# Moving the weight sums, the last batch's close, the memory tokens' split and two orders in a hybrid decoder layer

## The chip, the core and the metric

The kernel runs on one core of one Trainium2 chip. The metric is the device time of one execution in microseconds (us), the median of several runs. The engines are named as the profile does: PE is TensorE (PEld its weight loads), DVE is VectorE, ACT is ScalarE, POOL is GpSimd, SP is SyncE, whose queue issues most DMAs. "L825" is line 825 of the kernel before.

## What is computed

One layer of a decoder for 1024 prompt tokens and 8 sample requests of 4 tokens, each with 4096 cached tokens in 128-token pages. It has a mixer (gated MLP and latent attention side by side, one output projection), a cross-attention into 256 memory tokens, and a gated ConvFFN:

```python
def mla_keys_values(ckv_n, kpe, pos, w_uk, w_uv, g_qk_k):
    lead = ckv_n.shape[:-1]
    k_nope = (ckv_n @ w_uk).reshape(*lead, MLA_HEADS, QK_NOPE)
    v = (ckv_n @ w_uv).reshape(*lead, MLA_HEADS, V_HEAD)
...
def merge_out(a_out, b_out, g_out_a, g_out_b, w_o):
    return jnp.concatenate([rms_norm(a_out, g_out_a), rms_norm(b_out, g_out_b)], axis=-1) @ w_o

def mem_kv(mem, g_mem_in, w_mk, w_mv, g_mk):
    n, m, _ = mem.shape
    hm = rms_norm(mem, g_mem_in)
    k = rms_norm((hm @ w_mk).reshape(n, m, MEM_HEADS, MEM_HEAD_DIM), g_mk)
    v = (hm @ w_mv).reshape(n, m, MEM_HEADS, MEM_HEAD_DIM)
    return k, v
...
def conv_ffn(h, buf, w_up, w_conv, b_conv, w_down):
    t = h.shape[1]
    gate, val = jnp.split(h @ w_up, 2, axis=-1)
    gpad = jnp.concatenate([buf.astype(gate.dtype), gate], axis=1)
    conv = b_conv + sum(gpad[:, j:j + t] * w_conv[j] for j in range(CONV_W))
    return (jax.nn.silu(conv) * val) @ w_down, gpad[:, t:]
```

Products are made to fp32 precision: each operand is split into a high and a low part ("h", "l"), and `mm3` multiplies high by high, low by high and high by low.

## The kernel before

**Stages.** By the trace: input projections to about 200 us; attention over the prompt (`phase2a`) to 418; attention of the sample requests over their pages (`phase2b`) to 883; the memory keys (`mem_kv`) with the last request's softmax and output to 927; the output projection to 1100; memory attention to 1190; the ConvFFN to 1873.

**Prompt attention.** It has 16 units (head h, half G of the tokens), cut into 56 steps t. Tables say which side work is recorded in which step: `extra[t]` holds the splits of raw weights (`split_w`), the preparations of heads (`preps`: ropes on POOL, L609 to L612, the k addition L910, transposes L933), projections that come late, the sample queries' preparation (`sample_prep`: memsets of bdq and cn on POOL, L1039 and L1040, ahead of a copy of cn on ACT and its transposes on PE, L980), the output normalisation of the prompt (`mix`) and the 26 weight sums. PE, ACT, DVE and POOL run in the order that the tables give; SP's order comes from the scheduler.

**Weight sums.** The ConvFFN multiplies two-by-two blocks with seven products, which needs sums of weight blocks. `weight_sums` (L812) makes them ahead of time: load 512 KB (L817 or L822), four subtractions and additions on POOL (L825 to L828), store 512 KB (L829). Four sums take `w_up`, 22 take `w_down`. All use two buffers "wsum", which first hold the raw `w_uq` and `w_uv` halves that `split_w` reads; a buffer takes its next load when its last reader is done. In the tables the sums stand at steps 7 to 11, 25 to 31 and 36 to 50.

**Sample attention.** Each step loads pages (cT on L1311, ck on L1315), and POOL's krq product (L1330) feeds the first scores. The last steps also hold `mem_split`: the first four of eight blocks of memory tokens are scaled and split (ACT L195, DVE L198) while pages are still worked on. `mem_kv` then splits the other four inside head 0 and makes the keys of four heads. Three functions close each request: `batch_out` twice and `batch_close`, which ends in an ACT copy into `olT` (L1483). Those of the last request are called from `end()`, within the output projection, after `mixed` has recorded the splits (mx1, mx2: ACT L195, DVE L198) of the mixer's output for column blocks 1 and 2.

**ConvFFN.** A gate block's product X is drained by DVE into z (L2114) and into G (L2138); the convolution's steps run on DVE (L2161, L2162) into cv.

Of the kernel before, what the change touches and what calls it, by code (L numbers as in the profile page):

```python
# [6 lines left out]
FR = mybir.dt.float32r  # L7
# [6 lines left out]
P = 128  # L14
# [140 lines left out]
class Net:  # L155
# [23 lines left out]
    def mm3(self, out, a, b, first=True, last=True):  # L179
# [4 lines left out]
        for i, (l, r) in enumerate(seq):  # L184
            self.nc.tensor.matmul(out, l, r, start=first and i == 0, stop=last and i == len(seq) - 1)  # L185

    def split(self, hi, lo, src, g=None, eng="act"):

        nc = self.nc
        if g is None:  # L190
            {"act": nc.scalar.copy, "pool": nc.gpsimd.tensor_copy, "dve": nc.vector.tensor_copy}[eng](hi, src)  # L191
            low = lambda: nc.vector.tensor_tensor(lo, src, hi, ALU.subtract)  # L192
        else:
            if eng == "act":
                nc.scalar.activation(hi, src, AF.Copy, scale=g)  # L195
            else:
                {"pool": nc.gpsimd, "dve": nc.vector}[eng].tensor_scalar(hi, src, g, None, ALU.mult)
            low = lambda: nc.vector.scalar_tensor_tensor(lo, src, g, hi, ALU.mult, ALU.subtract)  # L198
        if self.lows is None:
            low()  # L200
        else:
            self.lows.append(low)

    def flush(self):
# [443 lines left out]
    def phase2a(self):  # L648
# [68 lines left out]

        put(split_w, (4, 5, 6, 7))
        spread(tok_s, 4, 11)
# [402 lines left out]
    def phase2b(self):  # L1122
# [47 lines left out]
        at(last - 4, 3, lambda: self.split(*wk0, raws[0].rearrange("p (k n) -> p k n", k=8)))  # L1170
        mem0 = []

        def mem_split(k):
            if k % 2 == 0:
                x = self.t(p, [P, 4, 288], FR, "ck", 15).rearrange("p k n -> p (k n)")[:, :1024].rearrange("p (k z n) -> p k z n", k=2, z=2)
                mem0.extend((x[:, e, 0], x[:, e, 1]) for e in range(2))
            self.split(*mem0[k], raws[1].rearrange("p (k n) -> p k n", k=4)[:, k], self.col("g_mem_in", k))

        for k in range(4):
            at(last - 3 + k, 3, mem_split, k)  # L1180
        for b in range(NB):
# [22 lines left out]
        def steps(n0, n1):  # L1204
            for n in range(n0, n1):
# [6 lines left out]
                for k, dst, src in ((1, b4, self.b_dram), (16, self.fold4, I["c_fold4"]), (64, wuv, I["w_uv"])):  # L1212
                    if n == k:
                        self.tc.add_manual_dep(
                            nc.sync.dma_start(dst, src).ins, self.page_dma[-1].ins.name,
                            mybir.DependencyInfo(mybir.DependencyClass.NoSync, mybir.DependencyReason.DATA), reason="order",
                        )
                if n > last - 8 and n % 2 == 0 and len(raws) < 4:
# [29 lines left out]
        with tc.manual_schedule(engines={E.SP}):  # L1248
            self.close("ps3")
            for x in ("p3a", "p3c", "sq", "sm"):  # L1250
                self.close(x)
            self.wr = self.open("wr", bufs=3, side="right")
            self.wp = self.open("w", bufs=3, side="right")
            mem = self.mem_kv(raws, wk0, mem0)
            for f in late:
                f()
            for _ in range(12):
                next(mem)
            steps(last + 1, last + 16 + LAG)
            for _ in mem:  # L1260
                pass
        self.close("p3")

        def end():
            for f in tail:
                f()
            ps = self.t(ppt, [P, 512], F32, "m", 1)[:NS]
            for h in range(8):
                for k in range(2):
                    nc.tensor.matmul(  # L1270
                        ps[:, h * 64 : h * 64 + 64], self.olT[:, k, h].rearrange("p b t -> p (b t)"),
                        wuv[:, k, h * 64 : h * 64 + 64], start=k == 0, stop=k == 1,
                    )
# [3 lines left out]
        return end  # L1277

# [199 lines left out]
    def batch_close(self, p, pp, b, s):  # L1478
        nc = self.nc
        tp = s["tp"][:, :64]  # L1480
        for k in range(2):
            nc.tensor.matmul(tp[:, k * 32 : k * 32 + 32], s["oo"][:, k * P : k * P + P], self.fold4[:, :32], start=True, stop=True)
        nc.scalar.copy(self.olT[:, :, :, b], tp.rearrange("p (k h t) -> p k h t", k=2, h=8))  # L1483

# [14 lines left out]

    def mem_kv(self, raws, wk0, mem0):  # L1500

# [5 lines left out]
        st = self.t(pp, [P, 512], F32, "st", 1)  # L1507
        mh, ml = (self.t(p, [P, 4, 256], FR, x) for x in ("mh", "ml"))
# [114 lines left out]

    def mixed(self):

# [464 lines left out]
    def ffn_up(self, ops, rows, norm, first):  # L2090
# [40 lines left out]
        def gate(w, fs, h, prev):  # L2131
# [24 lines left out]
            for e, f in enumerate(fs):  # L2156
# [176 lines left out]
def build(tc, I, O, stop=99, tap=None):  # L2333
# [22 lines left out]
    if done(2):  # L2356
        return
    end = N.phase2b()
    if done(3):
        return  # L2360
    mxs, ws = N.mixed()
    xp = N.open("x", side="right")
# [49 lines left out]
```

## Time and profile before

| what | us |
|---|---|
| median of 3 runs | 1878.63 |
| lowest and highest | 1877.48, 1888.89 |
| the profiled execution | 1874.82 |
| its span in the profile | 1873.1 |
| PE busy in the span | 1816.2 |
| DVE, ACT, POOL busy | 1347.5, 927.7, 693.9 |

By stage, from windows of the trace:

| stretch, us | PE busy | granted clock |
|---|---|---|
| 0 to 200 | 196.44 | 1.00 |
| 200 to 428 | 200.64 | 0.93 |
| 428 to 883 | 451.07 | 0.99 |
| 883 to 927 | 36.23 | 0.92 |
| 927 to 1100 | 170.04 | 0.99 |
| 1100 to 1190 | 85.83 | 1.00 |
| 1190 to 1873 | 675.95 | 1.00 |

A stretch's length less PE's busy time is idle time of PE; a granted clock below 1 means that its matmuls ran slower for a part of the stretch. The stretches with the most of both are the second and the fourth.

### The profile page before, as it was taken

Reading aid. Unit: us, or ns where it says so; the run is one execution under the profiler, and the core shown is the slowest. Engines: PE = TensorE matmul, PEld = TensorE weight load, DVE = VectorE, ACT = ScalarE, POOL = GpSimd, SP = SyncE. Lnnn points to the kernel's source line nnn. Section 1 sums busy time; section 2 is a strip of 40 time slices with the busy share of each in tenths; the row PEclk is TensorE's granted clock in tenths of the full one; section 3 lists DMA queues with packets and bytes.
Section 4 is the critical chain, followed back from the end, with each engine's and each line's share of the span. In section 5 each row is a group of like instructions: output and inputs, shape, how many; then the busy total and the mean of one; then the engine's idle time right before and its main releaser. Section 6 shows DMA issues by size and latency. Waiting matters only on the chain.

```text
span 1873.1 us, 39347 instructions
## 1 busy us (share of the span) xinstructions
PE 1816.2 (97%) x14222; PEld 1710.1 (91%) x14222; DVE 1347.5 (72%) x2796; ACT 927.7 (50%) x1965; POOL 693.9 (37%) x850
## 2 busy tenths in 40 slices
PE   9999899888999999998899999999999999999999
PEld 8999677658999999998799988899999999999999
DVE  7855666555887667777644676888888888878664
ACT  7436677555555555555433455633333333344442
POOL 1022244544444444544213110267776677500000
PEclk9999999798999999999999999999999999999999
DMA  8101042578776676664554345422222222495242
GB/s 322 38 25 66 21 136 82 191 239 233 217 199 188 176 199 185 171 177 141 153 160 134 127 158 151 132 67 80 81 83 90 69 74 75 114 350 166 79 154 76
DMA packets 153187, 261.18 MB, mean 139 GB/s; under 512 B 20897, under 2 KB 97538, under 8 KB 152994
## 3 DMA queue, kind: packets, MB, share of 16 engines
q1 hardware_dynamic: 152130, 257.63, 44.6%
q8 instruction: 112, 1.84, 0.4%
q10 hardware_dynamic: 864, 1.05, 0.2%
q14 instruction: 81, 0.66, 0.1%
HBM read 212.79 MB, written 45.82 MB: 138 GB/s over the span
## 4 chain that ended last, share of the span: by engine, by line
PE 76%; issue 6%; DMA 5%; SPq 4%; DVE 4%; POOL 3%; ACT 1%; DVEq 0%; POOLq 0%; ACTq 0%
PE s L185 12%; PE d L185 12%; PE mm L185 9%; PE b L185 7%; PE F L185 7%; PE X L185 7%; PE E L185 7%; PE A L185 3%; PE y L185 3%; SPq L1311 2%; SPq L1315 2%; PE o L995 1%; PE tp L185 1%; PE tp L980 1%; DMA wsumd<-wsum 1%
## 5 line engine op out<-in xcount | busy, mean ns | idle before, releaser
L185 PE MATMUL s<-w2h,ch 128*128 128x288 f32 (+1 forms) x1024 | 304.7, 298 | 0.5 <-ACT S L1361 0.5
L185 PE MATMUL s<-w2h,cl 128*128 128x288 f32 (+1 forms) x1024 | 296.8, 290 | 3.3 <-POOL cl L1343 3.3
L185 PE MATMUL s<-w2l,ch 128*128 128x288 f32 (+1 forms) x1024 | 295.5, 289 | 0.0
L185 PEld LDWEIGHTS s<-w2h,ch 128*128 128x128 f32 x1024 | 193.6, 189 | 8.9 <-ACT sq L1383 2.5
L185 PEld LDWEIGHTS s<-w2h,cl 128*128 128x128 f32 x1024 | 193.2, 189 | 5.4 <-POOL cl L1343 5.4
L185 PEld LDWEIGHTS s<-w2l,ch 128*128 128x128 f32 x1024 | 193.8, 189 | 0.0
L1386 DVE TENSOR_REDUCE ss<-sq 128x16 f32<-128x1024 f32 x128 | 155.3, 1213 | 32.5 <-ACT sq L1383 32.1
L1343 POOL TENSOR_TENSOR cl<-cT,ch 128x512 fp32r<-128x512 f32 x64 | 82.8, 1294 | 128.0 <-ACT ch L1339 127.1
L1383 ACT ACTIVATE sq<-s 128x512 f32<-128x512 f32 x128 | 76.5, 598 | 89.3 <-PE s L185 89.3
L1380 ACT ACTIVATE sq<-s 128x512 f32<-128x512 f32 x128 | 76.7, 599 | 73.6 <-PE s L185 72.7
L191 ACT CAST a<-brb 128x528 fp32r<-128x528 f32 x77 | 48.8, 634 | 112.9 <-PE d L185 108.5
L185 PE MATMUL d<-a,w 128*128 128x264 f32 x768 | 95.4, 284 | 1.2 <-DVE G L2185 1.2
L192 DVE TENSOR_TENSOR a<-brb,a 128x528 fp32r<-128x528 f32 x77 | 54.2, 705 | 57.4 <-ACT a L191 57.4
L185 PEld LDWEIGHTS d<-a,w 128*128 128x128 f32 x768 | 94.3, 188 | 1.3 <-issue 1.3
L2055 POOL TENSOR_TENSOR lo<-s,hi 128x1024 fp32r<-128x1024 f32 x20 | 62.8, 3142 | 45.4 <-ACT hi L2054 45.4
L185 PE MATMUL mm<-wlo,xh 128*128 128x256 f32 (+3 forms) x272 | 77.0, 286 | 0.1
L185 PE MATMUL mm<-whi,xh 128*128 128x256 f32 (+3 forms) x272 | 77.0, 285 | 0.0
L185 PE MATMUL mm<-whi,xl 128*128 128x256 f32 (+3 forms) x272 | 76.9, 287 | 0.0
L2110 ACT COPY a<-A 128x264 f32<-128x264 f32 x43 | 16.1, 374 | 118.8 <-PE A L185 113.9
L1339 ACT CAST ch<-cT 128x512 fp32r<-128x512 f32 x128 | 73.4, 626 | 0.0
L185 PE MATMUL d<-a,hi 128*128 128x264 f32 x552 | 72.0, 284 | 0.0
L1382 DVE TENSOR_TENSOR S<-s,S 128x64 f32<-128x64 f32 x128 | 28.0, 219 | 60.5 <-ACT sq L1380 60.4
(757 smaller groups left out, 6402.2 us busy)
## 6 DMA issues: line engine op xcount, KB each, us to landing
cT<-cT SPq DMA_DIRECT2D x256, 160.0 KB, 2.9
ck<-ck SPq DMA_DIRECT2D x256, 144.0 KB, 3.5
raw<-w_up SPq DMA_DIRECT2D x44, 512.0 KB, 3.6
wsumd<-wsum SPq DMA_DIRECT2D x26, 512.0 KB, 3.4
actd<-cv SPq DMA_DIRECT2D x44, 264.0 KB, 2.4
brb<-actd SPq DMA_DIRECT2D x44, 264.0 KB, 5.6
wsum<-w_down SPq DMA_DIRECT2D x22, 512.0 KB, 3.9
raw<-wsumd SPq DMA_DIRECT2D x20, 512.0 KB, 3.7
```

Of the source, the lines that this page charges most:

```text
L185: self.nc.tensor.matmul(out, l, r, start=first and i == 0, stop=last and i == len(seq) - 1)
L191: {"act": nc.scalar.copy, "pool": nc.gpsimd.tensor_copy, "dve": nc.vector.tensor_copy}[eng](hi, src)
L192: low = lambda: nc.vector.tensor_tensor(lo, src, hi, ALU.subtract)
L1311: dmas.append([nc.sync.dma_start(cT[:, j], I["cT"][bass.ds(rv, 1)].rearrange("a p n -> (a p) n")) for j, rv in enumerate(rvs)])
L1315: nc.sync.dma_start(ck[j * 32 : j * 32 + 32], I["ck"][bass.ds(rv, 1)].rearrange("a t s f -> (a t) s f"))
L1339: nc.scalar.copy(d["h"][:, k], src[k])
L1343: (nc.vector if k else nc.gpsimd).tensor_tensor(d["l"][:, k], src[k], d["h"][:, k], ALU.subtract)
L1380: nc.scalar.activation(sq[:, 0], ps[:, :, n0 : n0 + 256], AF.Square)
L1382: nc.vector.tensor_tensor(S, ps[:, :, sc : sc + 32], S, ALU.add)
L1383: nc.scalar.activation(sq[:, 1], pt.rearrange("p (e d) -> p e d", e=2), AF.Square)
L1386: yield lambda: nc.vector.tensor_reduce(s["ss"][:, g0 : g0 + 2].rearrange("p e (z h) -> p z e h", z=2), sq.rearrange("p z e (h d) -> p z e ...
L2055: eng.tensor_tensor(lo, src, hi, ALU.subtract)
```

## The change

Six edits.

1. The sums' steps are given as a tuple; the first groups are nine, five and twelve instead of five, seven and fourteen, and gaps are left between them.
2. `split_w` runs at steps 3 to 6, in the order q0, v0, q1, v1 instead of 4 to 7 in the order q0, q1, v0, v1.
3. `mix` gives up its turn at other places.
4. `mem_split` goes; `mem_kv` splits all eight blocks in head 0.
5. The last request's three closing functions are called in `mixed`, ahead of column block 2; the ACT half of that block's splits is ordered behind the copy into `olT`.
6. In the first half of the first gate block, the convolution's first step on DVE is ordered behind the drain of X into G.

```diff
-        put(split_w, (4, 5, 6, 7))
+        put(split_w[::2] + split_w[1::2], (3, 4, 5, 6))
...
-        times = [*range(7, 12), *range(25, 32), *(36 + j * 16 // 14 for j in range(14))]
+        times = (5, 6, 8, 9, 10, 12, 13, 14, 16, 25, 26, 27, 29, 30, 36, 37, 38, 40, 41, 42, 44, 45, 46, 48, 49, 50)
...
-                if k not in (0, 2):
+                if k not in (0, 2, 8):
+                    yield
+                if k == 4:
                     yield
...
-        for k in range(4):
-            at(last - 3 + k, 3, mem_split, k)
...
-            mem = self.mem_kv(raws, wk0, mem0)
+            mem = self.mem_kv(raws, wk0)
...
         def end():
-            for f in tail:
-                f()
...
-        nc.scalar.copy(self.olT[:, :, :, b], tp.rearrange("p (k h t) -> p k h t", k=2, h=8))
+        self.last_out = nc.scalar.copy(self.olT[:, :, :, b], tp.rearrange("p (k h t) -> p k h t", k=2, h=8))
...
-        xs = mem0 + [(mh[:, k], ml[:, k]) for k in range(4)]
+        xs = [(mh[:, k], ml[:, k]) for k in range(8)]
...
-                if h == 0 and k > 3:
+                if h == 0:
                     self.split(*xs[k], mr[k // 4][:, k % 4], self.col("g_mem_in", k))
...
             for c, (o, n) in enumerate(CH):
+                if c == 2:
+                    for f in tail:
+                        f()
...
-                        self.split(*(x[:, k + e, :w] for x in mxs[c]), raw[:, e], self.col("g_ab", k + e))
+                        hi = self.split(*(x[:, k + e, :w] for x in mxs[c]), raw[:, e], self.col("g_ab", k + e))
+                        if c == 2:
+                            self.behind(hi, self.last_out)
...
-                    nc.vector.tensor_tensor(G[:, 0, 2:n], ps, z, ALU.add)
+                    self.drain = nc.vector.tensor_tensor(G[:, 0, 2:n], ps, z, ALU.add)
...
-                nc.vector.scalar_tensor_tensor(c[:, :m], g[:, 1 : 1 + m], wc[1], c[:, :m], ALU.mult, ALU.add)
+                x = nc.vector.scalar_tensor_tensor(c[:, :m], g[:, 1 : 1 + m], wc[1], c[:, :m], ALU.mult, ALU.add)
+                if fs[0] == h == 0:
+                    self.behind(x, self.drain)
```

`behind(a, b)` is new: it adds an order between two instructions, a after b, that carries no data. Lines move by some places, so that L825 of before is L834 after, and so on.

On POOL at the memset of cn, before: the last subtractions of two sums, the memsets of the sample queries' tiles (bdq, cn) and the next sum. The first number behind "wsum" names the buffer's use.

```order
L827 TENSOR_TENSOR wsum_4392<-wsum_4392 128x256
L828 TENSOR_TENSOR wsum_4392<-wsum_4392 128x256
L825 TENSOR_TENSOR wsum_4432<-wsum_4432 128x256
L826 TENSOR_TENSOR wsum_4432<-wsum_4432 128x256
L827 TENSOR_TENSOR wsum_4432<-wsum_4432 128x256
L828 TENSOR_TENSOR wsum_4432<-wsum_4432 128x256
L1039 MEMSET bdq_4457 128x64
L1039 MEMSET bdq_4459 128x64
L1039 MEMSET bdq_4461 128x64
L1039 MEMSET bdq_4463 128x64
L1040 MEMSET cn_65 128x258
```

After, at the same memset:

```order
L837 TENSOR_TENSOR wsum_4391<-wsum_4391 128x256
L834 TENSOR_TENSOR wsum_4413<-wsum_4413 128x256
L835 TENSOR_TENSOR wsum_4413<-wsum_4413 128x256
L836 TENSOR_TENSOR wsum_4413<-wsum_4413 128x256
L837 TENSOR_TENSOR wsum_4413<-wsum_4413 128x256
L1048 MEMSET bdq_4471 128x64
L1048 MEMSET bdq_4473 128x64
L1048 MEMSET bdq_4475 128x64
L1048 MEMSET bdq_4477 128x64
L1049 MEMSET cn_65 128x258
```

The sum in front of the memset is the 12th before and the 14th after. Ahead of that, the first q rope stands behind five sums before and behind nine after; between the second k addition and the second rope of the sample queries there are three sums in both, and then four sums before and two after up to the memset.

On SP around the first twelve cT loads of the sample attention, before (the cT loads between are left out as are its register instructions):

```order
L817 DMA wsum_5053<-w_down 128x4x256
...
L1311 DMA cT_5097<-cT 128x320
L829 DMA wsumd_77<-wsum_4943 128x4x256
...
L1311 DMA cT_5139<-cT 128x320
...
L829 DMA wsumd_77<-wsum_5053 128x4x256
...
L1311 DMA cT_5181<-cT 128x320
...
L817 DMA wsum_5211<-w_down 128x4x256
L817 DMA wsum_5254<-w_down 128x4x256
...
L829 DMA wsumd_77<-wsum_5211 128x4x256
```

After:

```order
L838 DMA wsumd_77<-wsum_4950 128x4x256
...
L838 DMA wsumd_77<-wsum_5060 128x4x256
...
L1305 DMA cT_5104<-cT 128x320
...
L1305 DMA cT_5146<-cT 128x320
...
L1305 DMA cT_5188<-cT 128x320
...
L826 DMA wsum_5218<-w_down 128x4x256
L826 DMA wsum_5261<-w_down 128x4x256
...
L838 DMA wsumd_77<-wsum_5218 128x4x256
```

The loads behind the cT loads are those of the 21st and 22nd sums before, and of the 22nd and 23rd after. The stores of sums 19 and 20 stood among the cT loads; now the store of the 21st stands ahead of all of them.

On ACT at the close of the last request, before (mx1h and mx2h are the high parts of column blocks 1 and 2, oo and olT belong to the close):

```order
L1466 COPY oo_15002<-o_14685 128x257
...
L195 ACTIVATE mx1h_14923<-raw_14957,cols_58 128x384 x2
...
L195 ACTIVATE mx2h_14918<-raw_14963,cols_58 128x288 x2
L195 ACTIVATE mx2h_14918<-raw_14969,cols_58 128x288 x2
L195 ACTIVATE mx2h_14918<-raw_14975,cols_58 128x256 x2
L195 ACTIVATE mx2h_14918<-raw_14981,cols_58 128x256 x2
L1483 COPY olT_5594<-m_15004 128x16x4
```

After:

```order
L1460 COPY oo_14961<-o_14683 128x257
...
L201 ACTIVATE mx1h_14921<-raw_14955,cols_58 128x384 x2
...
L1477 COPY olT_5594<-m_14963 128x16x4
L201 ACTIVATE mx2h_14916<-raw_14971,cols_58 128x288 x2
L201 ACTIVATE mx2h_14916<-raw_14977,cols_58 128x288 x2
L201 ACTIVATE mx2h_14916<-raw_14983,cols_58 128x256 x2
```

The copy into olT moves from behind the eight activations of mx2h to ahead of them.

On the other engines, in words. On DVE four splits of memory tokens leave the last two pairs of page steps; behind the last reduction L1386 come a low part of `w_mk` and the eight low parts of memory tokens, where before there were four. PE interleaves the keys of heads 0 and 1. In the ConvFFN z and the drain into G stand ahead of two convolution steps L2161 that stood ahead of them.

More of the change, by code (lines that the diff above doesn't have):

```diff
@@ L185, in mm3, with behind @@
             self.nc.tensor.matmul(out, l, r, start=first and i == 0, stop=last and i == len(seq) - 1)
+    def behind(self, a, b):
+        self.tc.add_manual_dep(
+            a.ins, b.ins.name, mybir.DependencyInfo(mybir.DependencyClass.NoSync, mybir.DependencyReason.DATA), reason="order"
+        )
     def split(self, hi, lo, src, g=None, eng="act"):
-        nc = self.nc
+        nc, first = self.nc, None
         if g is None:
@@ L194, in split @@
             if eng == "act":
-                nc.scalar.activation(hi, src, AF.Copy, scale=g)
+                first = nc.scalar.activation(hi, src, AF.Copy, scale=g)
             else:
@@ L202, in split @@
             self.lows.append(low)
+        return first
     def flush(self):
@@ L1170, in phase2b @@
         at(last - 4, 3, lambda: self.split(*wk0, raws[0].rearrange("p (k n) -> p k n", k=8)))
[L1171 to L1177, printed above, removed]
-        for k in range(4):
-            at(last - 3 + k, 3, mem_split, k)
         for b in range(NB):
@@ L1213, in steps @@
                     if n == k:
[L1214 to L1217, printed above, removed]
+                        self.behind(nc.sync.dma_start(dst, src), self.page_dma[-1])
                 if n > last - 8 and n % 2 == 0 and len(raws) < 4:
@@ L1275, in end @@
             nc.scalar.copy(self.b_s, ps)
-        return end
+        return tail, end
     def batch_open(self, p, b):
@@ L1498, in stream, with mem_kv @@
         return hi, lo
-    def mem_kv(self, raws, wk0, mem0):
+    def mem_kv(self, raws, wk0):
         nc, tc, I, O = self.nc, self.tc, self.I, self.O
@@ L1621, in mix_steps, with mixed @@
                 yield
-    def mixed(self):
+    def mixed(self, tail):
         nc, I = self.nc, self.I
@@ L2357, in build @@
         return
-    end = N.phase2b()
+    tail, end = N.phase2b()
     if done(3):
         return
-    mxs, ws = N.mixed()
+    mxs, ws = N.mixed(tail)
     xp = N.open("x", side="right")
```

2 lines of the change are left out of this document (1 added, 1 removed).

## The prediction

> **What bounds the kernel now.** I read the page first, then the list of TensorE's waits, then the timelines around each of these waits, then the windows of 5 us with the granted clock.
>
> The page gives the busy share of TensorE (PE), and the list of waits gives, for each pair of waiting line and releasing line, the total, the number of times and the longest, all in us:
>
> ```profile
> PE 1816.2 (97%) x14222; PEld 1710.1 (91%) x14222; DVE 1347.5 (72%) x2796; ACT 927.7 (50%) x1965; POOL 693.9 (37%) x850
> ...
> PE s L1358 <- POOL krq L1330: 10.1, 1, 10.1
> ...
> PE b L185 <- DVE ck L198: 5.4, 2, 4.0
> ...
> PE m L1270 <- ACT olT L1483: 3.0, 1, 3.0
> ...
> PE X L185 <- DVE z L2114: 1.6, 1, 1.6
> ```
>
> TensorE is the bound: the change leaves its matmuls as they are, so it can only win back idle time and time at a lowered clock. With the wait of 5.63 for cn, which the next view shows, these make 25.7 us, and all five stand at places that the change touches. The timeline of TensorE (start, duration, line, out<-in, the wait in brackets) and the windows (PE, PEld, DVE, ACT and POOL busy, then the granted clock, DMA share, GB/s) show what the waits bring with them:
>
> ```profile
> 343.31 0.90 PE L980 MATMUL tp<-ident,pr 128*128 128x128 f32 x3 [5.63 <-ACT cn L1049]
> ...
> 360.46 1.06 PE L980 MATMUL tp<-ident,pr 128*128 128x128 f32 x4
> ...
> 369.29 0.88 PE L980 MATMUL tp<-ident,pr 128*128 128x128 f32 x6
> ...
> 427.94 0.80 PE L1358 MATMUL s<-bd,krq 128*128 128x128 f32 x2 [10.11 <-POOL krq L1330]
> ```
> ```profile
> 355.00:360.00 5.00, 5.00 (x19) 3.57 (x18) 2.68 (x10) 1.00 (x4) 2.81 (x4) 0.50 0.36 90
> 430.00:435.00 5.00, 5.00 (x31) 5.00 (x30) 1.29 (x3) 1.28 (x3) 3.72 (x6) 0.68 0.84 229
> 895.00:900.00 5.00, 5.00 (x46) 5.00 (x44) 1.00 (x2) 2.31 (x7) 4.67 (x10) 1.00 0.63 203
> 940.00:945.00 5.00, 5.00 (x29) 4.83 (x27) 2.09 (x11) 2.24 (x5) 0.00 (x0) 0.82 0.69 215
> ```
>
> The rows at 343.31, 360.46 and 369.29 begin two attention units of the same shape, heads 5 and 6 of the first half. The first takes 17.15 us, the second 8.83: behind its 5.63 us of idling the first runs at a granted clock of 0.50. So the cn wait costs 5.63 + 8.32 = 13.95 us, not 5.63. After the wait of 10.11 us (which begins at 417.83) the clock is still 0.68 on average in 430 to 435, and after the olT wait 0.82.
>
> **The weight sums, their pacing, and split_w (term A).** GpSimd (POOL) is in order, and the 26 sums stand in its queue between what TensorE waits for. Its timeline, with those of VectorE, SyncE's queue and TensorE at the places that matter:
>
> ```profile
> 241.30 0.73 POOL L825 TENSOR_TENSOR wsum<-wsum 128x256 f32<-128x256 f32 x1 [34.46 <-DMA wsum<-w_up]
> ...
> 251.31 0.74 POOL L825 TENSOR_TENSOR wsum<-wsum 128x256 f32<-128x256 f32 x1 [1.74 <-DMA wsum<-w_up]
> ...
> 259.45 0.73 POOL L825 TENSOR_TENSOR wsum<-wsum 128x256 f32<-128x256 f32 x1 [4.98 <-DMA wsum<-w_up]
> ...
> 262.58 0.74 POOL L825 TENSOR_TENSOR wsum<-wsum 128x256 f32<-128x256 f32 x1
> ...
> 283.20 1.05 POOL L910 TENSOR_TENSOR k<-kr,hr 128x512 f32<-128x512 f32 x1 [8.38 <-DVE hr L236]
> ...
> 286.66 1.84 POOL L609 TENSOR_TENSOR rp<-q,tq_c 128x256 f32<-128x256 f32 x1
> ...
> 326.52 0.73 POOL L825 TENSOR_TENSOR wsum<-wsum 128x256 f32<-128x256 f32 x1
> ...
> 342.55 0.31 POOL L1040 MEMSET cn<- 128x258 f32 x1
> ...
> 366.47 0.72 POOL L825 TENSOR_TENSOR wsum<-wsum 128x256 f32<-128x256 f32 x1 [1.89 <-DMA wsum<-w_down]
> ...
> 396.65 0.73 POOL L825 TENSOR_TENSOR wsum<-wsum 128x256 f32<-128x256 f32 x1 [9.50 <-DMA wsum<-w_down]
> ...
> 423.34 0.72 POOL L825 TENSOR_TENSOR wsum<-wsum 128x256 f32<-128x256 f32 x1 [3.25 <-DMA wsum<-w_down]
> ...
> 427.43 0.46 POOL L1330 TENSOR_TENSOR krq<-krq,krq 128x128 f32<-128x128 f32 x1
> ```
> ```profile
> 229.88 0.54 DVE L192 TENSOR_TENSOR wql<-wsum,wqh 128x384 fp32r<-128x384 f32 x1
> ...
> 236.81 0.43 DVE L192 TENSOR_TENSOR wvl<-wsum,wvh 128x256 fp32r<-128x256 f32 x1
> ```
> ```profile
> 381.51 5.95 SPq L1311 DMA_DIRECT2D cT<-cT  x7
> ...
> 391.80 0.99 SPq L817 DMA_DIRECT2D wsum<-w_down  x2
> ```
> ```profile
> 293.71 0.64 PE L933 MATMUL tp<-ident,k 128*96 128x128 f32 x4
> ```
>
> The rows of the sums are the 1st, 3rd, 4th, 5th, 10th, 17th, 21st and 26th. One sum is four subtractions of about 0.73, some 3 us of GpSimd; 241.30 to 262.58 is four spacings of 5.32, 396.65 to 423.34 is five of 5.34, so the pace is set by load, four subtractions, store through two buffers, not by GpSimd.
>
> *The start.* The first buffer came free with the third split, at 237.24. In the new order its two splits are the first two, one step sooner as well, which is the place of the split that ends at 230.4: 6.8 us sooner, so the first sum starts at 234.5. Nine sums now stand ahead of the first q rope instead of five. At 5.32 the ninth ends at 234.5 + 8 x 5.32 + 3.2 = 280.3. Behind it wait two ropes and the k addition; k and one rope took 3.46 (283.20 to 286.66), so all three about 5.9, to 286.2. TensorE needs that k at 293.71: 7.5 us of cover, gone if the spacing exceeds 6.27. That is where this edit can hurt: the ropes are queued behind the sums on GpSimd, and TensorE's unit waits for the ropes.
>
> *The middle.* Sums 10 to 14 stand where the 6th to 10th stood, and the memset of cn comes behind the 14th, at the place of the 10th's end, 326.52 + 3.2 + 0.4 = 330.1, where it came behind the 12th, at 342.55. TensorE gets there at 343.31 - 5.63 = 337.68 and needs 0.76 from memset to matmul: 330.9, in time by 6.8. So 13.95 goes, and TensorE would be through with prompt attention at 417.83 - 13.95 = 403.9. Next late are pr and the mask work, below 1.1 us each.
>
> *The end.* Sums 15 to 21 stand where the 11th to 17th stood; the 21st ends at 366.47 + 3.2 = 369.7. SyncE then issues its store and all twelve cT loads, 12 x 0.85 = 10.2 by the row of seven, and the loads of sums 22 and 23 go at 380.4 instead of 391.80. In before six sums were left at that point, to 426.06, or 34.3 us; now five, 34.3 - 5.3 = 28.9, so the chain ends at 409.3, and TensorE gets krq 1.9 later as before (427.94 - 426.06): 411.2. That is 16.7 sooner, with 7.3 us of idling left. The repacing of the mix steps and their two stores lies inside that idle time: nothing. Without that cover it would show as whatever delay one step has, under 2 us by the waits of 1.1 above.
>
> The bounds of A: if SyncE's cT loads end where they do now, loads 22 and 23 still go at 391.80 and A is 427.94 - 422.6 = 5.3. If GpSimd is wholly out of the way, TensorE starts at 403.9, A is 24.0, and the stretch of lowered clock after it (estimate 2.5, from the 0.68 in one window and the 2 us before it at half) goes too: 26.5. I take 16.7, because each step of it stands on rows of the same chain.
>
> The clock here is weighed against a rule. The row says 0.50 for a whole unit after 5.63 of idling. The Trainium skill, "TensorE: Matmul & The Clock Gate", section "The HAM clock gate", puts the return to the full clock at one busy window of about 3.4 us; by that only some 2 us of the 8.32 would belong to the wait (estimate: half of 3.4) and the rest would stay, TensorE would be ready at about 410, the sum would be the same since GpSimd comes at 411.2, but rival (1) below would give 1850 at best. The trace of before disagrees with that figure: 17 us at half clock.
>
> **Memory tokens (term C).** Four splits leave the last steps of the page loop, and eight now run at the start of mem_kv:
>
> ```profile
> 880.92 1.87 DVE L198 SCALAR_TENSOR_TENSOR ck<-ck,cols,ck 128x256 fp32r<-128x256 f32 x1
> ...
> 885.60 0.48 DVE L198 SCALAR_TENSOR_TENSOR ck<-ck,cols,ck 128x256 fp32r<-128x256 f32 x1
> 885.99 1.22 DVE L1386 TENSOR_REDUCE ss<-sq 128x16 f32<-128x1024 f32 x1
> ...
> 905.91 1.23 DVE L192 TENSOR_TENSOR lo<-raw,hi 128x1024 fp32r<-128x1024 f32 x1 [0.23 <-ACT hi L191]
> ```
> ```profile
> 880.95 1.56 POOL L1404 TENSOR_TENSOR S<-S,ss 128x768 f32<-128x768 f32 x1 [1.01 <-DVE ss L236]
> ```
> ```profile
> 883.62 0.50 PE L185 MATMUL b<-ck,wk0h 128*128 128x256 f32 x2
> ...
> 896.79 0.40 PE L185 MATMUL b<-ck,hi 128*128 128x256 f32 x2
> ```
>
> Before, TensorE's memory keys of heads 0 and 1 run from 883.62 to 896.79 with 5.44 of waiting, so 7.7 of work. Without the splits of 1.87 and 0.48 ahead of it the last reduction ends at the earliest 2 us sooner than 887.2, at 885.2, or unchanged. Then come a low part of w_mk (1.23) and the first ml (0.48): 886.9 to 888.9. Behind it lie 48 matmuls: 5.2 us at the full clock (46 of this kind in 5 us, 895 to 900) to the 7.7 of before. They can follow at once, since the two heads are now interleaved and each token feeds twice as many matmuls. The end lies at 892.1 to 896.6: a gain of 0.2 to 4.7; I take 2.5, the middle. What speaks against it is the first pair of rows: the split took 1.87 where GpSimd's addition ran at the same time, and 0.48 alone. The Trainium skill, "SBUF — State Buffer", section "SBUF: two separate sides", calls this an exclusive lock held for the whole instruction; were each of eight splits behind such an addition, C would be about -2 and the time 1858. Two additions stand near, so I keep 2.5.
>
> **The tail of the last batch (term D) and the order in the ConvFFN (term E).**
>
> ```profile
> 936.61 0.91 ACT L195 ACTIVATE mx2h<-raw,cols 128x256 fp32r<-128x256 f32 x2 [1.56 <-DMA raw<-mix]
> 937.42 0.19 ACT L1483 COPY olT<-m 128x64 f32<-128x64 f32 x1
> ```
> ```profile
> 1215.79 0.42 DVE L2114 TENSOR_TENSOR z<-X,a 128x264 f32<-128x264 f32 x1
> ```
>
> The copy of olT stands behind activations that wait for a DMA; now it is ahead of them. The wait of 2.96 goes, and with it the lowered clock of 940 to 945 (0.18 x 5 = 0.9): 3.9, from 0 (if TensorE then waits for mx2h, which is late by its DMA in any case) to 3.9. In the first half of the ConvFFN z and the drain pass two convolution steps on VectorE; the 1.6 of waiting goes. E is 1.6, at worst 0.
>
> **Sum.** 16.7 + 2.5 + 3.9 + 1.6 = 24.7. The profiled execution took 1874.8, so 1850.1 on its basis. The median of the runs is 1878.6, 3.8 above it; on that basis 1853.9. I predict 1854.
>
> **The rivals.** (1) *GpSimd gets out of the way altogether*: cT goes while sums run, TensorE starts the sample part at 403.9. 26.5 + 8.0 = 34.5, so 1844. For it speaks that GpSimd idles between sums; against it the pace of 5.3, which is held over all 26. (2) *The cT loads stay where they are*, because their buffers or the page table come free with TensorE's progress: 5.3 + 8.0 = 13.3, 1865. For it: in before they go out at 381.51 with nothing visible ahead of them. (3) *The packed early chain runs at the spacing of 251.31 to 259.45*, 8.14: GpSimd's ropes are late by 8 x (8.14 - 6.27) = 15.0, everything behind moves by as much, A is 1.7, total 9.7, 1869. (4) *Slower: the same queue at the spacing of the 21st sum*, 3.2 + 9.50 = 12.7, if the early loads queue as those did behind other loads on SyncE: late by 8 x (12.7 - 6.27) = 51, total 24.7 - 51 = -27, 1905. It loses from 24.7 = 8 x (p - 6.27), a spacing of 9.4, on. Against it: the early stretch has w_up loads and little else.
>
> **Chances.** Forecast 0.62 (own range 1846 to 1860), (1) 0.13, (2) 0.12, (3) 0.08, (4) 0.05. About 1% (18.8 us) is what a measurement of this kernel can tell from no change. Faster by more: 0.61 + 0.13 = 0.74. Within: 0.01 + 0.12 + 0.08 = 0.21. Slower: 0.05. The range from 1842 to 1866 takes in the forecast, (1) and (2), 0.87 of it, less their own ends.
>
> **What would show it.** Right: no wait for cn; clock 1.0 through head 5's unit; the first sum near 234.5 and the ninth by 282; loads of the 22nd near 380; TensorE's first sample matmul near 411 with about 7 us of waiting for krq; no wait for ck, olT or z beyond 1 us, and one for ml of about 3.5. Wrong: a wait of the units at 290 for k or q; cT at 380 or later; the half clock in head 5's unit without a wait; a new wait for mx2h near 937.

## The result, and the profile after

| | kernel before | changed kernel |
|---|---|---|
| median of 6 runs each, us | 1876.97 | 1862.41 |
| lowest to highest | 1872.85 to 1888.89 | 1859.94 to 1865.51 |
| profiled execution | 1874.82 | 1862.46 |
| its span | 1873.1 | 1860.8 |

The ratio is 0.9919, with a 95% interval of 0.9889 to 0.9948: faster by 14.6 us, or 0.8%. That lies in the forecast range and under the forecast gain of 24.7; by the prediction's bound of 1% it is "within", to which it gave a chance of 0.21. Both kernels were profiled a second time later (1876.30 and 1861.55), which matters below.

The list of TensorE's waits of the changed kernel (total, times, longest, in us):

```profile
PE s L1352 <- POOL krq L1324: 13.2, 3, 11.2
...
PE b L185 <- DVE ml L204: 2.8, 1, 2.8
...
PE tp L942 <- ACT pth L991: 1.6, 1, 1.6
...
PE b L185 <- ACT sq L1521: 1.5, 1, 1.5
```

The waits for cn, for ck, for olT and for z are gone; ml takes 2.8 where ck had 5.4. But the wait for krq (GpSimd, L1330 before, L1324 now) has grown from 10.1 to 13.2, and comes three times instead of once (9.2 and 12.2 in the second profiles of the two kernels). Two waits that were not there before, pth and (below) hsq, stand near 230 us. The timeline of TensorE at the start of the sample part, and the window in which head 5's unit ran at half clock before:

```profile
422.06 0.80 PE L1352 MATMUL s<-bd,krq 128*128 128x128 f32 x2 [11.21 <-POOL krq L1324]
```
```profile
355.00:360.00 5.00, 5.00 (x36) 4.16 (x35) 2.84 (x12) 4.37 (x12) 0.75 (x2) 1.00 0.64 210
```

The clock of 0.50 in 355 to 360 is now 1.00. The start of the sample part has moved from 427.94 to 422.06 and not to 411.

To see where time was won and lost, I read the start of the same instructions in both profiles of both kernels. "k" is the eighth group of transposes of k, "b_all" the last transposes of prompt attention, "krq" the first scores of the sample part, "cl first" and "cl last" the first and last of 64 products cl on GpSimd that run through the sample part, "qsq" the first square of the memory queries, "lo" ScalarE's last cast into the tile lo, near the kernel's end.

| mark, us | before | after | before, second profile | after, second profile |
|---|---|---|---|---|
| k | 255.41 | 261.75 | 258.05 | 260.43 |
| b_all | 417.23 | 410.25 | 421.82 | 407.98 |
| krq | 427.94 | 422.06 | 431.43 | 419.59 |
| cl first | 427.85 | 421.96 | 431.33 | 419.49 |
| cl last | 868.75 | 865.62 | 870.86 | 863.75 |
| qsq | 1033.42 | 1022.97 | 1035.08 | 1020.91 |
| lo | 1838.17 | 1825.81 | 1839.66 | 1824.91 |

Differences between neighbouring marks, first pair and second pair of profiles, changed less before:

| stretch | first pair | second pair | forecast |
|---|---|---|---|
| up to k | +6.3 | +2.4 | 0 |
| k to b_all | -13.3 | -16.2 | -13.95 |
| b_all to cl first | +1.1 | +2.0 | -2.8 |
| cl first to cl last | +2.8 | +4.7 | 0 |
| cl last to qsq | -7.3 | -7.1 | -6.4 (C and D) |
| qsq to lo | -1.9 | -0.6 | -1.6 (E) |

So terms C and D together came out at about their size, and so did the middle of term A; E did by these marks, but its stretch varies more than that from run to run (see the runs with one edit undone). Three stretches of A are wrong: the start, the end of the chain, and a stretch of which the prediction said nothing, the sample part's first 40 us.

*The start.* The timelines of ScalarE and TensorE of the changed kernel:

```profile
230.85 0.51 ACT L197 CAST wqh<-wsum 128x384 fp32r<-128x384 f32 x1 [4.57 <-PE tp L185]
```
```profile
232.38 0.64 PE L942 MATMUL tp<-ident,q 128*96 128x128 f32 x4 [1.56 <-ACT pth L991]
...
234.97 0.44 PE L1017 MATMUL tp<-ident,oc 128*128 128x128 f32 x2 [1.07 <-ACT hsq L892]
```

The first cast of split_w waits 4.57 us for TensorE: wqh still holds the first half's query weights, and the sample queries' products (wqh by cqh) have to read them first. They are recorded at step 4, so a cast recorded at step 3 stands still until these products are done, and with it everything behind it in ScalarE's queue: kTh, pth, pr. TensorE then waits for pth and hsq, 2.6 together.

*The chain and SyncE.* GpSimd's sums (the 1st, 9th, 21st, 22nd and 26th, with the k addition and the memset of cn), and SyncE's queue:

```profile
240.22 0.73 POOL L834 TENSOR_TENSOR wsum<-wsum 128x256 f32<-128x256 f32 x1 [32.75 <-ACT wvh L197]
...
286.37 0.73 POOL L834 TENSOR_TENSOR wsum<-wsum 128x256 f32<-128x256 f32 x1 [3.46 <-DMA wsum<-w_down]
...
295.31 1.04 POOL L919 TENSOR_TENSOR k<-kr,hr 128x512 f32<-128x512 f32 x1
...
337.60 0.31 POOL L1049 MEMSET cn<- 128x258 f32 x1
...
376.67 0.73 POOL L834 TENSOR_TENSOR wsum<-wsum 128x256 f32<-128x256 f32 x1 [4.44 <-DMA wsum<-w_down]
...
397.01 0.73 POOL L834 TENSOR_TENSOR wsum<-wsum 128x256 f32<-128x256 f32 x1 [17.17 <-DMA wsum<-w_down]
...
417.46 0.72 POOL L834 TENSOR_TENSOR wsum<-wsum 128x256 f32<-128x256 f32 x1 [2.06 <-DMA wsum<-w_down]
```
```profile
380.72 9.85 SPq L1305 DMA_DIRECT2D cT<-cT  x12
390.61 0.98 SPq L826 DMA_DIRECT2D wsum<-w_down  x2
...
422.65 1.20 SPq L1613 DMA_DIRECT2D mix<-q  x1
428.07 1.90 SPq L1309 DMA_DIRECT2D ck<-ck  x4
```

The first sum is 5.7 later than forecast, the 21st 10.2 (376.67 for 366.47), and the train of cT loads, which is 9.85 long as forecast, then ends at 390.6 and not 380.4. Behind it stand the loads of both buffers, and GpSimd idles for 17.17 us. The memset of cn at 337.60 was still in time.

*After the start.* Behind the 26th sum's store SyncE issues the stores of the mixer's output, and the first ck loads stand still until mix<-q has landed. The list of waits of SyncE's queue from 405 to 500, of the changed kernel:

```profile
SPq L1309 <- DMA mix<-q: 4.0, 1, 4.0
```

Before, SyncE's list of waits for that stretch had no such entry (0.2 us in the second profile): mix<-q was issued at 419.47, ahead of the last two sums' stores, and ck at 427.11. So the pages come 1 us later than before, though TensorE starts 5.9 sooner.

### The profile page after: what moved, and what is told of

The parts are those of the page before. It is cut to its first block, busy times and chain, and to the rows that moved or that the text cites. A ratio compares the mean times of both kernels' runs of the same rounds, so it can differ in the third digit from the quotient of the medians.

```text
span 1860.8 us, 39348 instructions
## 1 busy us (share of the span) xinstructions
PE 1808.0 (97%) x14222; PEld 1703.1 (92%) x14222; DVE 1351.3 (73%) x2796; ACT 926.8 (50%) x1965; POOL 696.5 (37%) x850
## 4 chain that ended last, share of the span: by engine, by line
PE 78%; issue 6%; DMA 5%; SPq 4%; DVE 3%; ACT 2%; POOL 2%; POOLq 0%; DVEq 0%; ACTq 0%
PE s L185 12%; PE d L185 12%; PE mm L185 9%; PE b L185 8%; PE F L185 7%; PE X L185 7%; PE E L185 7%; PE A L185 3%; PE y L185 3%; SPq L1305 2%; DMA cT<-cT 2%; PE o L1004 1%; SPq L1309 1%; PE tp L185 1%; PE tp L989 1%
## 5 line engine op out<-in xcount | busy, mean ns | idle before, releaser
L2175 POOL TENSOR_TENSOR cv<-cv,row 128x1056 f32<-128x1056 f32 x22 | 65.1, 2958 | 21.0 <-ACT cv L2174 21.0
```

What stands on the lines that cost most here:

```text
L2175: nc.gpsimd.tensor_tensor(cv, cv, row, ALU.mult)
```

## The experiments

In all of them the marks of the table above are read from the run's own profile, and the ratio is that of the timed runs to the kernel before.

**Edits 4 to 6 alone.** The sums, the splits and the mix are as before:

```diff
-        put(split_w[::2] + split_w[1::2], (3, 4, 5, 6))
+        put(split_w, (4, 5, 6, 7))
...
-        times = (5, 6, 8, 9, 10, 12, 13, 14, 16, 25, 26, 27, 29, 30, 36, 37, 38, 40, 41, 42, 44, 45, 46, 48, 49, 50)
+        times = [*range(7, 12), *range(25, 32), *(36 + j * 16 // 14 for j in range(14))]
...
-                if k not in (0, 2, 8):
-                    yield
-                if k == 4:
+                if k not in (0, 2):
                     yield
```

> The changed kernel with edits 1 to 3 undone (sums, splits and mix as before); memory tokens, last close and ConvFFN order as changed. Theory (what the two traces show, place by place): these three give 2.6 + 4.7 + 1.9 = 9.2 us against the kernel before, about 1866 on the profiled basis, and the first three edits together are worth only the remaining 3. Rival (the record's sum): the three give 8.0 and the sums' edits 16.7, of which something later takes 13 back; then this run shows 8.0 or less, and the start of the sample part stays at 427.9. Second rival: the three lean on the sums' edits, and alone give under 5.

The ratio is 0.9970 (0.9955 to 0.9986), 5.6 us below before (4.2 by the medians, 1871.29 and 1875.49). In its profile the time from cl last to lo is 962.67, against 969.42 and 968.80 in the two of before: 6.1 to 6.8. The theory's 9.2 was too much, the prediction's 8.0 as well, but neither is far off; the remaining 0.5% of the change, some 9 us by medians, belongs to edits 1 to 3, which no run here tells apart. The second rival (under 5) is not excluded by the interval. The start of the sample part does not stay at 427.94: in this profile it is at 435.09, after a wait of 16.0 for krq. Its sums are late from the first (247.31, where the two profiles of before have 241.30 and 244.02) to the 26th (430.48, where they have 423.34 and 426.84), so one profile of this chain is uncertain by several us.

**Splits one step later.**

```diff
-        put(split_w[::2] + split_w[1::2], (3, 4, 5, 6))
+        put(split_w[::2] + split_w[1::2], (4, 5, 6, 7))
...
-        times = (5, 6, 8, 9, 10, 12, 13, 14, 16, 25, 26, 27, 29, 30, 36, 37, 38, 40, 41, 42, 44, 45, 46, 48, 49, 50)
+        times = (5, 7, 8, 9, 10, 12, 13, 14, 16, 25, 26, 27, 29, 30, 36, 37, 38, 40, 41, 42, 44, 45, 46, 48, 49, 50)
```

> The changed kernel with the four weight splits one step later (steps 4 to 7, in the new order) and the second sum at step 7. Theory: in step 3 the cast into wqh has to wait until TensorE has read the old wqh for the sample queries, and ScalarE's queue stands behind it; one step later that wait of 4.57 us goes, TensorE wins 2.5 to 3 us before 260, and as the later sums are tied to TensorE's progress the total falls by about 3 against the changed kernel (to 1859). Rival: the wait is hidden, since TensorE waits for GpSimd's chain at the start of the sample part in any case and the chain hangs on DMA alone: then the total stays within 1 of the changed kernel, or rises by up to 3 if the first buffer comes free later.

ScalarE's timeline shows the same cast with the wait of before the change, and the waits for pth and hsq are not in TensorE's timeline:

```profile
229.53 0.51 ACT L197 CAST wqh<-wsum 128x384 fp32r<-128x384 f32 x1 [0.97 <-PE tp L185]
```

k is reached at 257.85, where the two profiles of the changed kernel have 261.75 and 260.43, so 2.6 or more are back in this profile. (Of the three later profiles with the same later splits two have 256.53 and 256.83, but the third has 262.44, without the waits and with a lower clock between 210 and 235.) But the ratio is 0.9948 (0.9927 to 0.9969), no better than the changed kernel's. The sample part starts at 420.17, between the changed kernel's 422.06 and 419.59. The rival holds: what TensorE wins here it then waits for, since the chain with its 16 us gap behind cT is late in any case.

**cT loads behind the last sum's load.** The order is given to SyncE by one more call of `behind`; the two multiplications of the tables are recorded ahead of the loads, and the loads twelve turns later.

```diff
...
+        n = len(self.page_dma)
         self.quads = {Q: self.quad_load(None, Q) for Q in range(3)}
+        self.behind(self.page_dma[n], self.sum_loads[25])
```

> The changed kernel with the first twelve cT loads ordered behind the load of the 26th sum (and the two multiplications of the cosine tables recorded ahead of them). Theory: the loads of the 22nd and 23rd sums stand in SyncE's queue behind the train of cT loads, which leaves GpSimd idle for 17 us; without it the chain ends about 12 us sooner, TensorE starts the sample part at about 411 to 413 instead of 422, and the total falls by 7 to 10 against the changed kernel. Rival: the pace of load, sum and store does not carry on because cT then collides with them, or the first scores wait for cT: gain below 3, or a loss of up to 5.

The first scores of this run:

```profile
409.92 0.46 PE L1357 MATMUL s<-bd,krq 128*128 128x128 f32 x2 [0.81 <-DVE b_last L1022]
```

TensorE no longer waits for the chain at all: 409.92 instead of 422.06. That part of the theory is shown. The time from cl first to cl last, however, is 448.1, where the changed kernel has 443.7 and 444.3 and before 440.9 and 439.5. SyncE shows why:

```profile
414.00 0.90 SPq L1618 DMA_DIRECT2D mix<-q  x1
418.96 1.87 SPq L1314 DMA_DIRECT2D ck<-ck  x4
```

The ck loads start 9 us after TensorE, since they wait for mix<-q. Of the 9.7 to 12.1 us won at the start against the two profiles of the changed kernel, 3.9 to 4.5 go there. The ratio is 0.9881 (0.9844 to 0.9919), or 1855.98 in the median, 6.4 below the changed kernel's median, with intervals that overlap.

**Both.** The last two edits together.

> Both edits of the two runs before at once. Theory: with GpSimd's chain out of the way TensorE's progress is the bound up to the sample part, so the 2.5 to 3 us of the split show in full on top: 10 to 13 below the changed kernel, about 1850. Rival: page loads bind the first 40 us of the sample part whatever starts it, and the gain stays at half of that.

krq is at 407.11, 2.8 sooner than with the cT edit alone, which fits the split's 2.6; but the same kernel profiled once more (below) has 414.00, so this single difference shows nothing yet. cl last is at 854.16 instead of 857.58. The profiled execution took 1855.03, the median of the timed runs 1857.69, ratio 0.9895 (0.9860 to 0.9929). Up to the sample part's start this profile fits the theory; the total fell by 4.7 against the changed kernel's median, about the rival's half, with intervals that overlap.

**Mixer's stores first.** To test the page loads by themselves, on the changed kernel:

```diff
...
             assert not steps
+            for x in self.sum_stores[-2:]:
+                self.behind(x, self.mix_dma)
```

> The changed kernel with the stores of the 25th and 26th sums ordered behind the last store of the mixer's output on SyncE, so that the two stores into mix_dram go out when TensorE has finished the prompt attention and not behind the 26th sum. Theory: the start of the sample part at 422 stays, but the first ck loads go out about 6 us sooner (421 to 422 instead of 428), since they wait for the last of these stores, and the 2.75 us that TensorE loses again between 445 and 465 come back: 2.5 to 3 below the changed kernel. Rival: the loss between 445 and 465 is the DMA engines' own pace (0.7 to 0.9 busy there) and not the start of the loads: no more than 1 us.

The ck loads start at 420.65, and GpSimd's waits from 430 to 470 change. In the changed kernel:

```profile
POOL krq L1322 <- DMA cT<-cT: 20.2, 5, 6.3
POOL cl L1337 <- ACT ch L1333: 6.2, 3, 4.1
```

With the mixer's stores first:

```profile
POOL cl L1339 <- ACT ch L1335: 19.3, 6, 4.5
POOL krq L1324 <- DMA cT<-cT: 2.6, 3, 1.3
```

GpSimd waited for pages; now it waits for ScalarE, which follows TensorE. From cl first to cl last it takes 439.77 us, 3.9 to 4.5 less than the changed kernel and the same as before. So the loss is that of the page loads' start, as the theory has it. The total does not show it: 0.9916 (0.9883 to 0.9949). From cl last to qsq this profile takes 160.06, 2.7 to 2.9 more than the changed kernel, with a granted clock of 0.70 in 910 to 915, so part of the gain was lost again in that execution; whether it always is stays open.

**Edits 4, 5 and 6 undone one at a time.** Each is the changed kernel with the diff of that edit taken back.

> The changed kernel with edit 4 undone: four memory tokens split in the last page steps again. Theory: place by place the trace loses the 2.6 us that it won between the last page scores and the first memory keys, mainly the two waits for ck (5.4 in before) against one for ml (2.8): about 2.5 above the changed kernel. Rival: the gain there came from the interleaving of the next heads and not from these splits; or eight splits behind the last reduction cost as much as they save: within 1.

> The changed kernel with edit 5 undone: the last request's close is called from the output projection again. Theory: the wait of about 3 us for the copy into olT comes back, with up to 1 us of lowered clock: 3 to 4.5 above the changed kernel. Rival: the close fills idle slots of the memory keys' stage in either place, and with the memory tokens changed nothing waits for it any more: within 1.

> The changed kernel with edit 6 undone: the first convolution step of the first gate block may stand ahead of the drain again. Theory: the wait of TensorE for z of 1.6 us comes back, 1.6 to 2 above the changed kernel, all of it between 1195 and 1215. Rival: something else in the first gate block ends later anyway: 0.

The waits come back where they were, in each run's own list of TensorE's waits:

```profile
PE b L185 <- DVE ck L204: 5.4, 2, 4.0
```
```profile
PE m L1266 <- ACT olT L1479: 2.2, 1, 2.2
```
```profile
PE X L185 <- DVE z L2113: 1.7, 1, 1.7
```

| run | cl last to qsq | qsq to lo | ratio |
|---|---|---|---|
| changed kernel, two profiles | 157.35, 157.16 | 802.84, 804.00 | 0.9919 (0.9889 to 0.9948) |
| without edit 4 | 160.36 | 802.49 | 0.9943 (0.9920 to 0.9965) |
| without edit 5 | 159.33 | 802.28 | 0.9936 (0.9914 to 0.9957) |
| without edit 6 | 157.22 | 807.87 | 0.9932 (0.9907 to 0.9957) |

By these rows edit 4 is worth 3.0 to 3.2 in its stretch and edit 5 2.0 to 2.2. But from cl last to qsq the ten profiles here that keep both edits take 157.16 to 160.06, so what each is worth alone is not shown beyond the wait that it removes; both together are, against 164.22 and 164.67 before. For edit 6 the stretch is 3.9 to 5.0 longer, but most of that has another cause: 2.2 to 2.8 lie ahead of the ConvFFN's first matmul into X (t21h by hi), where the granted clock is 0.50 from 1100 to 1105. From that matmul to lo it takes 640.60 without edit 6 and 640.25 and 640.33 before; in the changed kernel's two profiles 638.37 and 638.96, and 637.94 to 638.75 in the six others that keep edit 6 and have no new wait there. So the edit is worth 1.3 to 2.7, as forecast. All three ratios lie above the changed kernel's, but none beyond the intervals.

**All three repairs.** Splits later, cT late and the mixer's stores first.

> The changed kernel with the splits one step later, the first cT loads behind the load of the 26th sum, and the stores of the mixer's output ahead of the last two sums' stores: all that the runs so far point to. Theory: TensorE starts the sample part at about 407 (21 sooner than before the change); since the ck loads wait for the mixer's last store in any case, whose data TensorE only has at 406, the third edit adds at most 1 to 2 to the second and the first, and the total is 18 to 22 below the kernel before, 5 to 9 below the changed one. Rival: page loads take back what the earlier start wins, and the total is that of the changed kernel within 3.

krq is at 409.33, cl last at 854.64, and the ratio 0.9910 (0.9896 to 0.9924). The third edit adds nothing to the second, as expected: the ck loads wait for data that TensorE has just made. The gain is below the theory's, 2.1 under the changed kernel's median, and the rival's bound of 3 holds. Two waits in TensorE's list that the changed kernel has not say where some of it went:

```profile
PE A L2014 <- DVE hr L243: 1.8, 1, 1.8
...
PE tp L945 <- POOL k L922: 1.4, 1, 1.4
```

The first stands at the start of the ConvFFN, in all three profiles that have late cT loads and later splits and in no other: there TensorE's order has the matmuls A ahead of a part of X, and the way from the first matmul into X to lo takes 641.12 to 642.92 in place of 638.4 to 639.0. Why the order differs there stays open. The second is the wait for the k addition behind nine sums, at 296.63, with a granted clock of 0.69 and 0.62 in the two windows from 295 to 305.

**Both kernels once more**, unchanged, each in one execution with a profile.

> The kernel before once more, as it is, for a second profile. Theory: the lowered clock between 205 and 220 that nearly all other profiles have and the first profile of this kernel has not is not the change's doing but falls differently in each execution; there is about an even chance to see it here, with 2 to 5 us lost by 255, and if it is seen the change is not its cause. Rival: it comes from the changed code; then this profile has none, with marks up to 255 within 1 us of the first profile.

> The changed kernel once more, as it is, for a second profile. Theory: the waits for pth and hsq near 230, the idle time of GpSimd behind the cT loads and the wait for the first krq come again within 1 us each, while the lowered clock between 205 and 220 may or may not. Rival: the 17 us of GpSimd's idling were that execution's, not the kernel's.

The window from 210 to 215 (the granted clock is the third number from the end) of before, first and second profile:

```profile
210.00:215.00 5.00, 4.59 (x25) 3.73 (x26) 3.95 (x13) 1.20 (x3) 0.00 (x0) 1.00 0.01 3
```
```profile
210.00:215.00 5.00, 4.48 (x14) 3.83 (x15) 3.23 (x10) 0.47 (x1) 0.00 (x0) 0.50 0.02 3
```

The lowered clock is not the change's doing: the second execution of before has it too, and reaches k at 258.05, 2.6 later than the first. Of the 6.3 that the first pair shows up to k, 2.4 are left between the second profiles, and these stand beside the 2.6 of waits for pth and hsq. (The run with edits 4 to 6 alone, which has the old splits and no such waits, reaches k at 261.34, so the marks alone do not show that the start costs anything; the waits do.) The second profile of the changed kernel has the 4.57 us of the cast, GpSimd's gap behind cT (16.02) and the wait for mix<-q (4.0) again.

**The best version once more.** Late cT loads and later splits, in more rounds.

> The kernel of the run with late cT loads and later splits once more, in more rounds, since its profile ended 19.8 us sooner than the first profile of before and its few timed runs only 17.8 sooner. Theory: 0.988 to 0.990 of the kernel before, 2 to 6 us below the changed one. Rival: what it wins ahead of the sample part is given back by the lowered clock and by waits in the later stages, and it stands with the changed kernel, 0.991 to 0.993.

Its profile is 8.7 us longer than the first one of the same kernel (1863.68 and 1855.03): k is at 262.44 instead of 256.53, krq at 414.00 instead of 407.11. The ratio is 0.9892 (0.9876 to 0.9909), 1859.21 in the median beside 1879.55 of before. It is faster than the kernel before beyond doubt; against the changed kernel (0.9919, to 0.9889 at the lower end) it is 0.3% better by the middle of the intervals, which overlap.

## Why the prediction came out as it did

The direction held, and so did the mechanism of the middle of A and of C, D and E. The range held by luck: the measured 1862.41 lies outside the forecast's own 1846 to 1860 and next to rival (2)'s 1865, and the range had been drawn wide enough to take that rival in. The forecast gain of 24.7 was too large by 10, and nearly all of that is term A: 16.7 was forecast, and by the marks from the start to cl last the two pairs of profiles show 3.1 and 7.1, around the 5.3 that the prediction named as the lower bound of A and as rival (2). C and D were 6.4 and came as 7.1 to 7.3; E was 1.6 and came as 1.9 and 0.6.

*The wait for cn and the half clock*: right, and the largest gain. The forecast of 13.95 stands beside 13.3 and 16.2. That the half clock belonged to the wait is seen from its absence: in all eleven profiles of kernels whose sums stand as in the changed kernel, or nearly so, the wait for cn is gone and the windows from 345 to 365 have a clock of 1.00; in the run with the sums as before the wait is back (5.4), and the clock is 0.50 in 350 to 355. By the Trainium skill, "TensorE: Matmul & The Clock Gate", section "The HAM clock gate", some 3.4 us of work should have brought the clock back, and the traces disagree: 18 us in the first profile of before and 25 in the second, with 0.50 in every window from 345 to 370.

*The start*: the step "the place of the split that ends at 230.4: 6.8 us sooner" failed. It took the split's place in the old order and left out that wqh must have been read before it is written again. The first sum came 1.1 sooner, not 6.8, and TensorE waited 2.6 for what stood behind the cast. The later splits remove these waits.

*The cover of 7.5 us ahead of the ropes*: it held only because TensorE was late as well. The k addition ended at 296.35, 10.2 later than forecast, and TensorE reached it at 300.04 instead of 293.71. The spacing of the first nine sums was (286.37 - 240.22)/8 = 5.77, below the 6.27 at which the prediction saw the cover gone. Where TensorE comes sooner the cover is gone: with later splits it waited for this k in two profiles of four, 1.43 us in the run with all three repairs and 0.35 in the best version once more. That is the "wait of the units at 290 for k" that the prediction gave as a sign of being wrong.

*The end of the chain*: the length of the cT train and its place were right, the time was not: "cT at 380 or later" was another sign of being wrong, and the train began at 380.72 (378.81 in the second profile). The 21st sum was 10.2 late, and 7.7 of that stood at the 14th (334.19, where the 10th of before has 326.52). The sums 13 and 14 stand behind the sample queries' rope, and that rope waited 10.08 us, by the trace for ScalarE's kTh, a copy of TensorE's transposes. The lateness of TensorE thus went through to the end, and the chain ended at 420.5, not 409.3. In the second profiles the 21st sum is 5.9 late (374.78, where the 17th of before has 368.89), so a part of the 10.2 is the quick first execution of before. Rival (2), in which cT binds the chain, named the right place, and its 422.6 for TensorE's start is what was measured (422.06), but for another reason than it gave: with cT ordered later the chain ran on at once (22nd sum at 381.18 instead of 397.01). A slip in the sum did no harm: the 26th sum of before ended at 426.46 and not at 426.06, which cancels against the 1.9 to krq.

*"The repacing of the mix steps and their two stores lies inside that idle time: nothing"*: wrong. The stores do lie in TensorE's idle time, but the page loads of the next stage stand behind them on SyncE. In SyncE's order the mixer's stores fell behind the sums' stores (whether by edit 1 or by edit 3 is not tested), and 2.8 to 4.7 of the gain went in the sample part's first 40 us. The run with these stores first shows it.

*Memory tokens, the close, the drain*: right, each with its wait; the wait for ml is 2.8, where about 3.5 was forecast. The eight splits took 1.31 for three and 3.49 for five (883.12 and 884.45 on VectorE), 0.44 to 0.70 each, the five beside three additions on GpSimd (885.11 to 887.66), so the contention with GpSimd that would have made C negative did not come.

## What to carry to other kernels

Before a copy is moved ahead in a queue, look for who still reads what it overwrites: an in-order engine that waits for that reader holds up all that stands behind it. Where a stage is made to end sooner, follow the next stage's loads through the same queue, for here they took 2.8 to 4.7 us of the gain back. And a mark read in two executions of the same unchanged kernel says how much of a difference between two profiles is the change's.

## What the runs showed of the hardware that was not expected

The granted clock falls to 0.50 to 0.74 in the window from 210 to 215 in ten of the fourteen profiles here (0.82 in one), although no wait of TensorE from 198 to 222 is longer than 1.7 us in the lists; three profiles (the first of before, the first with late cT loads and later splits, and the one with all three repairs) have 1.00 there with the same work, and 0.64 to 0.67 in the window from 200 to 205. The second profile of the kernel with late cT loads and later splits, with the very same instructions, has 0.69 in 210 to 215. After a wait of 5.4 to 5.6 us for cn the half clock lasted some 10 us (edits 4 to 6 alone), 18 us and 25 us (the two profiles of before). The two profiles of before differ by 2.6 us at k and by 4.6 at b_all, the two of the changed kernel by up to 2.5, and the two of the kernel with late cT loads and later splits by 5.9 at k and 8.7 at lo, which is a fair part of what this change is worth.
